# Three blocks of an MLP: the left half of the second product by seven block products in place of eight

## The chip, the core and the metric

The kernel runs on one core of one Trainium2 chip. The core has a matmul engine, TensorE (PE in the rows; its loads of stationary operands are PEld), VectorE (DVE), ScalarE (ACT), GpSimd (POOL) and SyncE (SP), whose queue issues most DMAs. Matmuls write into PSUM, which this program uses as eight banks of 128 x 512 float32; everything else lies in SBUF. Each engine takes its instructions in a fixed order and waits on semaphores for the others. The metric is the device time of one execution, in microseconds (us).

## What is computed

A two-layer encoder trunk over 256 tokens with 2048 features: in each layer attention, then a dense MLP with a squared ReLU, with 8192 hidden features.

```python
h = _rmsnorm(x) * (1.0 + sc_m) + sh_m
y = jnp.square(jax.nn.relu(h @ w_mlp_in[l])) @ w_mlp_out[l]
x = x + g_m * y
...
return _rmsnorm(x, final_norm_g)
```

The MLP of the second layer (l = 1) is the last thing before the closing norm. All values are float32.

## The kernel before

**Precision.** A float32 value is split into two float32r parts: `hi` is a rounding copy made by ACT (line 151, or 187 for activations), `lo` is the rest, which DVE makes with a subtraction (line 154, or 188). A float32 product is then three matmuls: hi x hi, hi x lo and lo x hi. Weights come from memory as float32 tiles of 128 x 2048 (`raw`, 1 MB, five buffers) and are split in two halves of 1024 columns into tiles `hi` and `lo`, which have four buffers each: a fifth half waits until the matmuls that read the first are done.

**The MLP of a layer** (end of `layer`) goes through four blocks `fb` of 2048 hidden features.

- First product: `wides` takes two tiles of 128 hidden features at a time. For each it makes 16 matmuls of 512 columns (line 217: one `hi` slice of the weights as the stationary operand, hi and lo parts of 256 tokens side by side as 512 columns), and then 16 of 256 columns (line 220: the `lo` slice on the hi parts). The two halves of the resulting bank are added by `joined` (ACT copies one, line 1201; DVE adds the other, line 1202). `relu2` applies relu and square on ACT (lines 1207 and 1208) and splits the result into `hid` (ACT line 187, DVE line 188), two tiles with hi and lo.
- Second product: `rows` computes a column of 512 output features for both halves of the tokens in two banks `pr`. It goes through four quarters `kq` of the 2048 hidden features; each is a `raw` tile and 24 matmuls of 512 columns (lines 311, 312 and 314, `hid` slices of 128 x 128 stationary, weights moving). Four columns c make a block.
- `updates` multiplies a column by the gate and adds it to x (DVE lines 1126 and 1128). In the last block of the second layer `final` does the same, sums squares on ACT (line 1142) and, after the last column, scales and stores the output.

In the second layer, block 0 has its first six hidden tiles from an earlier stage; blocks 1 to 3 are whole. All of the first product of a block comes ahead of its second product. The order of instructions on each engine is decided when the program is built, by a scheduler that starts from the order of the code; tiles take buffers from rotating pools. DMAs of weights are issued on SP's queue in the order of the code, each as soon as its buffer is free.

## Time and profile before

| | us |
|---|---|
| median of 3 runs (lowest to highest) | 2168.12 (2168.02 to 2169.72) |
| the profiled execution, its own time | 2169.38 |
| span of its trace | 2167.6 |
| first product of block 1 of the second layer | 1631.2 to 1720.1 |
| second product of that block | 1720.1 to 1807.2 |
| start of block 3 of the second layer | 1983.3 |
| last matmuls of the program | 2158 to 2159 |

A profile has one row for each group of instructions: the line of the code, the engine, the operation, the tile written <- the tiles read, shapes and count, then busy time and mean duration, then the idle time of the engine ahead of them and what ended it. A row of a timeline starts with the start in us and the length; in square brackets stands how long the engine had been idle and which instruction ended that. A row of windows gives for a stretch its length and then the busy us (and instructions) of PE, PEld, DVE, ACT and POOL, the granted clock of TensorE as a share of the full one, the busy share of the DMA engines and GB/s. Matmul durations include their latency, so successive ones overlap: their pace is read from starts.

### The profile page before, as it was taken

To read this page: it belongs to the slowest core of one execution; us is meant where nothing else is said; L and a number is where in the kernel's file an instruction comes from. 1 tells how busy PE (TensorE), PEld (TensorE's weight loads), DVE (VectorE), ACT (ScalarE), POOL (GpSimd) and SP (SyncE) were. 2 spreads that over 40 slices of the span, in tenths; PEclk is the share of its full clock that TensorE was granted. 3 is DMA by queue.
4 is the path that set the end of the run, shared out by engine and by line. 5 is a ranking of instruction groups with operands and counts; after the bars stand their busy time and mean duration, and the time that the engine had idled before them with its cause. 6 is when DMAs were issued, how large, how long until landed. Compare 5 with 4: busy or idle time off the path is not lost.

```text
span 2167.6 us, 29372 instructions
## 1 busy us (share of the span) xinstructions
PE 2140.6 (99%) x11498; PEld 1861.7 (86%) x11498; DVE 1593.9 (74%) x2122; ACT 1148.1 (53%) x1738; POOL 6.3 (0%) x18
## 2 busy tenths in 40 slices
PE   7999999999999999999999999999999999999998
PEld 6899888898888888888889998888888888888886
DVE  7888889888688888888877886778555555555555
ACT  6555663565455355445454576557535534644643
POOL 0000000000000000000000000000000000000000
PEclk9999999999999999999999999999999999999999
DMA  9998889799888988888967776767655555565552
GB/s 387 418 345 330 313 331 358 288 339 339 322 319 325 343 325 324 325 327 320 343 221 270 263 257 231 274 221 273 226 207 181 194 192 179 190 212 176 194 196 96
DMA packets 87244, 594.76 MB, mean 274 GB/s; under 512 B 9856, under 2 KB 10304, under 8 KB 20288
## 3 DMA queue, kind: packets, MB, share of 16 engines
q1 hardware_dynamic: 85968, 587.08, 73.7%
q0 software_dynamic: 848, 5.28, 0.6%
q8 instruction: 90, 1.47, 0.3%
q10 hardware_dynamic: 288, 0.52, 0.1%
q14 instruction: 50, 0.41, 0.1%
HBM read 589.66 MB, written 3.18 MB: 274 GB/s over the span
## 4 chain that ended last, share of the span: by engine, by line
PE 96%; DVE 2%; DMA 1%; ACT 1%; SPq 0%; issue 0%; ACTq 0%
PE ps L217 19%; PE pr L311 13%; PE pr L312 13%; PE pr L314 13%; PE ps L220 10%; PE pk L260 3%; PE pk L284 2%; PE pk L194 2%; PE pk L198 2%; PE pk L197 2%; PE pv L296 2%; PE pv L298 2%; PE pv L297 2%; PE psm L1372 1%; PE pk L281 1%; PE ps L197 1%
## 5 line engine op out<-in xcount | busy, mean ns | idle before, releaser
L154 DVE TENSOR_TENSOR lo<-raw,hi 128x1024 fp32r<-128x1024 f32 (+1 forms) x714 | 835.9, 1194 | 436.0 <-issue 225.2
L151 ACT ACTIVATE hi<-raw 128x1024 fp32r<-128x1024 f32 (+1 forms) x714 | 732.6, 1036 | 690.2 <-PE pr L312 365.3
L380 DVE SCALAR_TENSOR_TENSOR ada<-ada,cond 128x2048 f32<-128x2048 f32 x192 | 438.0, 2285 | 11.8 <-DMA ada<-in_w_ada 11.1
L217 PE MATMUL ps<-h,hi 128*128 128x512 f32 x1856 | 431.5, 390 | 0.0
L217 PEld LDWEIGHTS ps<-h,hi 128*128 128x128 f32 x1856 | 345.2, 188 | 69.4
L311 PE MATMUL pr<-hi,hid 128*128 128x512 f32 x1024 | 398.6, 389 | 0.0
L312 PE MATMUL pr<-hi,hid 128*128 128x512 f32 x1024 | 398.5, 389 | 0.0
L314 PE MATMUL pr<-lo,hid 128*128 128x512 f32 x1024 | 253.5, 389 | 0.0
L220 PEld LDWEIGHTS ps<-h,lo 128*128 128x128 f32 x1856 | 230.3, 192 | 4.5
L220 PE MATMUL ps<-h,lo 128*128 128x256 f32 x1856 | 231.7, 283 | 0.0
L314 PEld LDWEIGHTS pr<-lo,hid 128*128 128x128 f32 x1024 | 192.2, 188 | 39.9
L312 PEld LDWEIGHTS pr<-hi,hid 128*128 128x128 f32 x1024 | 192.2, 188 | 39.7
L311 PEld LDWEIGHTS pr<-hi,hid 128*128 128x128 f32 x1024 | 192.2, 188 | 39.7
L1201 ACT ACTIVATE sum<-ps 128x256 f32<-128x256 f32 x110 | 42.1, 383 | 114.8 <-PE ps L220 114.4
L194 PE MATMUL pk<-h,hi 128*128 128x256 f32 x320 | 90.4, 285 | 0.2 <-ACT h L705 0.2
L197 PE MATMUL pk<-h,hi 128*128 128x256 f32 x320 | 90.5, 283 | 0.0
L198 PE MATMUL pk<-h,lo 128*128 128x256 f32 x320 | 90.5, 283 | 0.0
L188 DVE TENSOR_TENSOR hid<-relu,hid 128x256 fp32r<-128x256 f32 x128 | 48.3, 421 | 49.5 <-ACT hid L187 49.5
L260 PE MATMUL pk<-hf,w 128*128 128x256 f32 x384 | 83.9, 379 | 0.0
L260 PEld LDWEIGHTS pk<-hf,w 128*128 128x128 f32 x384 | 72.8, 190 | 9.9
L194 PEld LDWEIGHTS pk<-h,hi 128*128 128x128 f32 x320 | 61.2, 192 | 0.6 <-ACT h L705 0.5
L198 PEld LDWEIGHTS pk<-h,lo 128*128 128x128 f32 x320 | 61.4, 192 | 0.2 <-DVE lo L154 0.2
(250 smaller groups left out, 2459.3 us busy)
## 6 DMA issues: line engine op xcount, KB each, us to landing
raw<-in_w_m SPq DMA_DIRECT2D x238, 1024.0 KB, 5.3
ada<-in_w_ada SPq DMA_DIRECT2D x192, 1024.0 KB, 6.4
raw<-in_w_o SPq DMA_DIRECT2D x32, 1024.0 KB, 5.5
raw<-in_w_m SPq DMA_DIRECT2D x24, 768.0 KB, 5.4
raw<-in_w_dv SPq DMA_DIRECT2D x16, 1024.0 KB, 5.5
raw<-in_w_t SPq DMA_DIRECT2D x12, 1024.0 KB, 5.8
w<-in_w_a SPq DMA_DIRECT2D x24, 384.0 KB, 13.5
raw<-in_w_a SPq DMA_DIRECT2D x12, 768.0 KB, 4.6
```

Of the source, the lines that this page charges most:

```text
L151: ins = self.nc.scalar.activation(hi, v, AF.Copy)
L154: ins = self.nc.vector.tensor_tensor(lo, v, hi.bitcast(F32), ALU.subtract)
L194: ins = mm(ps, hi, x[0], start=first, stop=False, skip_group_check=shared)
L197: mm(ps, hi, x[1], start=False, stop=False, skip_group_check=shared)
L198: self.last_mac = mm(ps, lo, x[0], start=False, stop=last, skip_group_check=shared)
L217: mm(ps.rearrange("p a b -> p (a b)"), part(w, k, 0), x[2], start=k == 0, stop=False)
L220: mm(ps[:, 0], part(w, k, 1), x[0], start=False, stop=k == nk - 1)
L260: self.nc.tensor.matmul(ps, v, whole[k], start=first, stop=last, skip_group_check=True)
L311: mm(ps, xh[:, c], part(i, 0), start=kq == 0 and i == 0, stop=False)
L312: mm(ps, xl[:, c], part(i, 0), start=False, stop=False)
L314: self.last_mm = mm(ps, xh[:, c], part(i, 1), start=False, stop=kq == 3 and i == 3)
L380: ins = nc.vector.scalar_tensor_tensor(w, w, 1.0, self.cond, ALU.mult, ALU.mult, accum_out=acc[:, i : i + 1])
```

## The change

Blocks 1 to 3 of the second layer's MLP run through a new function, `block_by_seven`. The right half of the second product (c = 2 and 3) stays as it was. The left half (c = 0 and 1), a product of tokens x hidden by hidden x 1024, is taken in blocks: two halves of the tokens, two tiles of 128 hidden features, two halves of 512 output features. A 2 x 2 by 2 x 2 block product takes eight block products as written; here it takes seven, of sums and differences of the blocks, summed over all hidden tiles in seven PSUM banks (`sums`, tiles `pp`), and `four` puts the four results together at the end of the block.

```diff
         for fb in range(NFB):
+            if l and fb:
+                self.block_by_seven(fb, h)
+                continue
...
+    def block_by_seven(self, fb, h):
+        io = self.io
+        hid, steps, sums = [], [], []
+        for m in range(0, NK, 2):
+            both = self.t("sum")
+            for j in range(2):
+                ps = self.wides([io["w_m11"][NK * fb + m + j - 6]], h)[0]
+                self.join(ps, both[:, j])
+                if steps:
+                    steps.pop(0)()
+            r = self.relu(both)
+            parts = self.split(r, "hid", True)
+            hid += parts
+            steps = self.seven(io["w_ms"][fb - 1, m // 2], parts, r, sums, m == 0, m == NK - 2)
+        for f in steps:
+            f()
+        end = fb == NFB - 1
+        for c, pss in enumerate(self.four(sums)):
+            (self.final if end else self.updates)(pss, c)
+        for c in range(2, 4):
+            pss = self.rows(io["w_m2"][1, fb], hid, c, end and c == 3)
+            (self.final if end else self.updates)(pss, c)
+
+    def seven(self, src, parts, r, sums, first, last):
...
+        s = flat(self.t("comb"))
+        (a11, a12), (a21, a22) = [[r[:, k, P * t : P * t + P] for k in range(2)] for t in range(2)]
+        q = [s[:, P * i : P * i + P] for i in range(4)]
+        add(q[2], a11, a21, ALU.subtract)
+        add(q[0], a21, a22, ALU.add)
+        add(q[1], q[0], a11, ALU.subtract)
+        add(q[3], a12, q[1], ALU.subtract)
+        hi, lo = flat(self.u("sh", F32R)), flat(self.u("sl", F32R))
+        nc.scalar.activation(hi, s, AF.Copy)
+        add(lo, s, hi.bitcast(F32), ALU.subtract)
...
+        def product(x, w, i, p):
+            ps = flat(sums[p - 1])
+            wh, wl = (v[:, 512 * i : 512 * i + 512] for v in w)
+            nc.tensor.matmul(ps, x[0], wh, start=first, stop=False)
+            nc.tensor.matmul(ps, x[0], wl, start=False, stop=False)
+            nc.tensor.matmul(ps, x[1], wh, start=False, stop=last)
+
+        def five():
+            if first:
+                sums.extend(self.bank("pp") for _ in range(7))
+            raw = self.raw(src, 2048)
+            comb = self.wp.tile([P, 2048], F32, tag="raw", name=self.name("comb"), bufs=5)
+            add(comb[:, :1024], raw[:, 512:1536], raw[:, :1024], ALU.subtract)
+            add(comb[:, 1024:1536], raw[:, 1024:1536], comb[:, :512], ALU.subtract)
+            add(comb[:, 1536:], comb[:, 1024:1536], raw[:, 1536:], ALU.subtract)
+            w = self.part(raw, 0, 512)[0]
+            product(h11, w, 0, 1)
+            w = self.part(raw, 1, 1024)[0]
+            product(h12, w, 1, 2)
+            product(s4, w, 0, 3)
+            w = self.part(comb, 0, 1024)[0]
+            product(s1, w, 0, 5)
+            product(s3, w, 1, 7)
+            st["comb"] = comb
+
+        def two():
+            w = self.part(st["comb"], 1, 1024)[0]
+            product(s2, w, 0, 6)
+            product(h22, w, 1, 4)
+
+        return [five, two]
+
+    def four(self, sums):
...
+        self.nc.scalar.activation(c11, p1, AF.Copy)
+        add(c12, p6, c11, ALU.add)
+        add(c11, p2, c11, ALU.add)
+        add(c21, p7, c12, ALU.add)
+        add(c12, p5, c12, ALU.add)
+        add(c22, p5, c21, ALU.add)
+        add(c12, p3, c12, ALU.add)
+        add(c21, c21, p4, ALU.subtract)
+        return [c11, c21], [c12, c22]
```

`joined` and `relu2` are taken apart into `join`, `relu` and `split`, and the weights of the left half are stored a second time in the new order (`w_ms`). A **step** m is one pass of the loop: the first product of two tiles, one tile at a time, with the "five" of the step before after the first tile and the "two" of the step before after the second. The last step's five and two come after the loop. Per step one `raw` tile of second-product weights is loaded, a tile `comb` of combined weights is made from it in another buffer of the same five, and four combinations of the activations are made and split (`sh`, `sl`). On PE the program has 10718 rows in place of 10790.

**A step in the middle, DVE.** Before, these rows stood around the joins of one pair of tiles in block 1 (`ps` the first product's bank, `lo` a low part of weights, `sum` the joined tile):

```order
L154 TENSOR_TENSOR lo_2722_14904<-raw_2720_14901,hi_2721_14903 128x1024
L154 TENSOR_TENSOR lo_2724_14908<-raw_2720_14901,hi_2723_14907 128x1024
L1202 SCALAR_TENSOR_TENSOR sum_2715_14886<-ps_2703_14800,sum_2715_14886 128x256
L154 TENSOR_TENSOR lo_2728_14915<-raw_2726_14912,hi_2727_14914 128x1024
L1202 SCALAR_TENSOR_TENSOR sum_2715_14886<-ps_2709_14811,sum_2715_14886 128x256
L154 TENSOR_TENSOR lo_2730_14919<-raw_2726_14912,hi_2729_14918 128x1024
```

Now, from the split of a step's combined weights to the join of the next step's second tile (`comb<-raw` is the making of the combined weights, `sl` the low part of the combined activations):

```order
L154 TENSOR_TENSOR lo_2811_15294<-comb_2805_15272,hi_2810_15293 128x1024
L1099 TENSOR_TENSOR sl_2796_15221<-comb_2794_15215,sh_2795_15220 128x512
L1295 SCALAR_TENSOR_TENSOR sum_2797_15224<-ps_2798_15225,sum_2797_15224 128x256
L154 TENSOR_TENSOR lo_2815_15307<-raw_2813_15304,hi_2814_15306 128x1024
L154 TENSOR_TENSOR lo_2817_15311<-raw_2813_15304,hi_2816_15310 128x1024
L154 TENSOR_TENSOR lo_2819_15349<-comb_2805_15272,hi_2818_15348 128x1024
L154 TENSOR_TENSOR lo_2830_15381<-raw_2828_15378,hi_2829_15380 128x1024
L1116 TENSOR_TENSOR comb_2834_15424<-raw_2833_15422 128x1024
L1117 TENSOR_TENSOR comb_2834_15424<-raw_2833_15422,comb_2834_15424 128x512
L1118 TENSOR_TENSOR comb_2834_15424<-comb_2834_15424,raw_2833_15422 128x512
L154 TENSOR_TENSOR lo_2832_15385<-raw_2828_15378,hi_2831_15384 128x1024
L1295 SCALAR_TENSOR_TENSOR sum_2797_15224<-ps_2812_15303,sum_2797_15224 128x256
```

The two joins of a pair were one row apart, with at most one split between; now eight rows of other work stand between them, and a whole step has 20 rows on DVE.

**The end of a block, ACT.** Before, at the end of block 1's first product (`hi<-raw` are splits of weights for the second product):

```order
L1201 ACTIVATE sum_2779_15286<-ps_2767_15200 128x256
L1201 ACTIVATE sum_2779_15286<-ps_2773_15211 128x256
L1207 ACTIVATE relu_2780_15291<-sum_2779_15286 128x512
L151 ACTIVATE hi_2796_15372<-raw_2795_15370 128x1024
L1208 ACTIVATE relu_2780_15291<-relu_2780_15291 128x512
L187 ACTIVATE hid_2781_15294<-relu_2780_15291 128x256
L187 ACTIVATE hid_2782_15295<-relu_2780_15291 128x256
```

Now, from the join of block 1's last tile (`pp_2681` is the first of the seven sums, `y` its copy, `sh` the high part of the combined activations):

```order
L1294 ACTIVATE sum_2855_15528<-ps_2870_15607 128x256
L151 ACTIVATE hi_2892_15713<-comb_2885_15682 128x1024
L1302 ACTIVATE relu_2878_15662<-sum_2855_15528 128x512
L1303 ACTIVATE relu_2878_15662<-relu_2878_15662 128x512
L187 ACTIVATE hid_2879_15665<-relu_2878_15662 128x256
L187 ACTIVATE hid_2880_15666<-relu_2878_15662 128x256
L1141 ACTIVATE y_2894_15723<-pp_2681_14655 128x512
L1098 ACTIVATE sh_2882_15676<-comb_2881_15671 128x512
L151 ACTIVATE hi_2905_15751<-raw_2904_15749 128x1024
```

On PE the last tile was followed by the second product's matmuls on the block's oldest `hid`; now it is followed by six matmuls of the step before and then by all 21 of the last step, on `hid_2879`, `hid_2880` and `sh_2882`, ahead of any of the right half:

```order
L1109 MATMUL pp_2684_14658<-hi_2876_15652,hid_2851_15514 128x512
L1107 MATMUL pp_2681_14655<-hi_2886_15686,hid_2879_15665 128x512
L1108 MATMUL pp_2681_14655<-lo_2887_15687,hid_2879_15665 128x512
L1109 MATMUL pp_2681_14655<-hi_2886_15686,hid_2879_15665 128x512
L1107 MATMUL pp_2682_14656<-hi_2888_15693,hid_2880_15666 128x512
L1108 MATMUL pp_2682_14656<-lo_2889_15694,hid_2880_15666 128x512
L1109 MATMUL pp_2682_14656<-hi_2888_15693,hid_2880_15666 128x512
```

Three more on `hid_2880` follow, then twelve on `sh_2882` and its low part, then the right half.

**The start of a block, ACT.** Now, from the join of block 1's second tile to the first combined activations (`hi_2698` and `hi_2700` are the two halves of the fourth tile's weights):

```order
L1294 ACTIVATE sum_2655_14500<-ps_2662_14546 128x256
L1302 ACTIVATE relu_2668_14591<-sum_2655_14500 128x512
L151 ACTIVATE hi_2694_14685<-comb_2689_14664 128x1024
L1303 ACTIVATE relu_2668_14591<-relu_2668_14591 128x512
L151 ACTIVATE hi_2698_14698<-raw_2697_14696 128x1024
L187 ACTIVATE hid_2669_14594<-relu_2668_14591 128x256
L187 ACTIVATE hid_2670_14595<-relu_2668_14591 128x256
L1294 ACTIVATE sum_2674_14609<-ps_2675_14610 128x256
L151 ACTIVATE hi_2700_14702<-raw_2697_14696 128x1024
L1098 ACTIVATE sh_2672_14605<-comb_2671_14600 128x512
```

Before, at the same place, relu, square and the two `hid` rows stood together with one split between, and nothing on PE read them until the second product. Now step 0's five, after the third tile, reads `hid_2669`, `hid_2670` and `sh_2672`.

More of the change, by code (lines that the diff above doesn't have):

```diff
@@ new lines, in four @@
+    def four(self, sums):
+        add = self.nc.vector.tensor_tensor
+        p1, p2, p3, p4, p5, p6, p7 = sums
+        c11, c12, c21, c22 = [self.t("y") for _ in range(4)]
+        self.nc.scalar.activation(c11, p1, AF.Copy)
[7 more added lines that the diff above has]
+        return [c11, c21], [c12, c22]
@@ L1199, in joined, with join, relu @@
         for i in range(2):
[L1200 to L1203 removed]
+            self.join(ps[i], out[:, i], scale)
+        return out
+    def join(self, ps, t, scale=1.0):
+        self.nc.scalar.activation(t, ps[:, 0], AF.Copy, scale=scale)
+        self.nc.vector.scalar_tensor_tensor(t, ps[:, 1], scale, t, ALU.mult, ALU.add)
     def relu2(self, ps):
+        return self.split(self.relu(ps), "hid", True)
+    def relu(self, ps):
         r = self.t("relu")
```

22 lines of the change are left out of this document (13 added, 9 removed).

## The prediction

> **What bounds the kernel now.** I read the shares of busy time first, then the chain that ended last, then the two stages that the change touches, one block of the second layer's MLP: first product from 1631.2 us, second product from 1720.1 us.
>
> ```profile
> PE 2140.6 (99%) x11498; PEld 1861.7 (86%) x11498; DVE 1593.9 (74%) x2122; ACT 1148.1 (53%) x1738; POOL 6.3 (0%) x18
> PE 96%; DVE 2%; DMA 1%; ACT 1%; SPq 0%; issue 0%; ACTq 0%
> ```
>
> ```profile
> 1631.20:1720.10 88.90, 88.90 (x514) 78.72 (x513) 49.19 (x66) 51.32 (x75) 0.00 (x0) 1.00 0.52 180
> 1720.10:1807.20 87.10, 87.10 (x386) 72.14 (x386) 46.60 (x49) 36.01 (x37) 0.00 (x0) 1.00 0.59 203
> ```
>
> In both stretches TensorE (PE) is busy for the whole time at a granted clock of 1.00, while VectorE (DVE) has 46 to 49 us of work in 87 to 89 and the DMA engines are half idle. Only matmuls taken away can save time here. Their pace stands in the chain:
>
> ```profile
> 1910.80 1.81 PE pr L314 x8
> 1916.24 1.81 PE pr L314 x8
> 1994.42 7.28 PE ps L217 x32
> 2001.70 3.83 PE ps L220 x32
> ```
>
> A quarter of a column of the second product, 24 matmuls of 512 columns, repeats every 1916.24 - 1910.80 = 5.44 us: **0.227 us each**. In the first product 512 columns take 7.28/32 = 0.2275 us and 256 columns 3.83/32 = 0.12 us, so one tile (16 + 16) takes 5.56 us.
>
> **What is removed.** The left half of the second product had 4 quarters x 24 x 2 columns = 192 matmuls a block; seven block products of three matmuls in eight steps are 168. 24 fewer in three blocks are 72 x 0.227 = **16.3 us less on PE**. All else must hide behind PE, or it comes off this.
>
> **What is added, and the middle of a block.** A step (two first-product tiles, then the "five" and "two" pieces of the seven products) takes PE 2 x 5.56 + 21 x 0.227 = 15.9 us. Durations for DVE and ScalarE (ACT):
>
> ```profile
> L154 DVE TENSOR_TENSOR lo<-raw,hi 128x1024 fp32r<-128x1024 f32 x244 | 291.8, 1220 | 249.0 <-issue 155.1 <-PE ps L220 86.9 <-ACT hi L151 7.0
> L188 DVE TENSOR_TENSOR hid<-relu,hid 128x256 fp32r<-128x256 f32 x64 | 24.2, 422 | 43.5 <-ACT hid L187 43.5
> L1202 DVE SCALAR_TENSOR_TENSOR sum<-ps,sum 128x256 f32<-128x256 f32 x58 | 24.2, 418 | 0.0
> L1128 DVE TENSOR_TENSOR x<-x,yg 128x512 f32<-128x512 f32 x33 | 21.6, 684 | 0.1
> L394 DVE TENSOR_TENSOR mod<-macc,vec 128x2 f32<-128x2 f32 x2 | 0.3, 156 | 0.0
> ```
>
> ```profile
> L151 ACT ACTIVATE hi<-raw 128x1024 fp32r<-128x1024 f32 x244 | 258.2, 1058 | 232.3 <-PE pr L312 181.3 <-PE ps L217 41.9 <-issue 5.2
> L187 ACT ACTIVATE hid<-relu 128x256 fp32r<-128x256 f32 x64 | 23.1, 410 | 0.9
> L1201 ACT ACTIVATE sum<-ps 128x256 f32<-128x256 f32 x58 | 22.3, 384 | 67.0 <-PE ps L220 66.9
> L1207 ACT ACTIVATE relu<-sum 128x512 f32<-128x512 f32 x32 | 20.2, 634 | 26.7 <-DVE sum L1202 26.7
> L1208 ACT ACTIVATE relu<-relu 128x512 f32<-128x512 f32 x32 | 19.6, 616 | 0.0
> ```
>
> The new 128-wide additions lie between 0.156 us (2 columns) and 0.422 (256); the line through both gives 0.29. The new 1024- and 512-wide subtractions are taken as L154 and L1128. A step then gives DVE seven splits and one subtraction of 1024 (9.76), four operations of 512 (2.76), four of 128 (1.16), two hid splits and two joins (1.68): **15.4 us of work in 15.9**. ACT gets seven splits, two of 512, two joins, relu, square and two hid: 11.5 us, which hides. What decides is whether DVE's operations overlap a little, and the price of a handover:
>
> ```profile
> 1701.58 0.72 ACT L187 ACTIVATE hid<-relu 128x256 fp32r<-128x256 f32 x2
> 1702.03 0.76 DVE L188 TENSOR_TENSOR hid<-relu,hid 128x256 fp32r<-128x256 f32 x2 [1.49 <-ACT hid L187]
> ...
> 1708.64 0.42 DVE L1202 SCALAR_TENSOR_TENSOR sum<-ps,sum 128x256 f32<-128x256 f32 x1
> 1708.97 1.22 DVE L154 TENSOR_TENSOR lo<-raw,hi 128x1024 fp32r<-128x1024 f32 x1
> 1709.04 7.44 PE L217 MATMUL ps<-h,hi 128*128 128x512 f32 x32
> 1709.24 0.38 ACT L1201 ACTIVATE sum<-ps 128x256 f32<-128x256 f32 x1 [1.54 <-PE ps L220]
> 1710.11 0.42 DVE L1202 SCALAR_TENSOR_TENSOR sum<-ps,sum 128x256 f32<-128x256 f32 x1
> ```
>
> DVE starts 1.14 us after a 1.22 us split began and 0.33 after a 0.42 us join: 0.08 less than the duration. ACT to DVE costs 0.04 (1701.58 + 0.41 to 1702.03). ACT reads a finished tile 0.20 us after PE has gone on (1709.04 to 1709.24).
>
> The seven sums hold seven of PSUM's eight banks, so a tile can start only when the join before it has emptied the last bank. From the start of a step's first tile: split buffers rotate by four, so the split of the combined weights waits for the buffer that this tile's low parts free at 3.64 + 0.96 + 0.20 = 4.80 us. With it twelve DVE operations stand up to the join of the second tile (their rows are in the part on the change): seven of 1.22, three of 0.69, two joins, 11.45 us end to end, 10.8 with nine overlaps of 0.08 and two dependent steps of 0.04. The join ends at 15.6, PE may go on at 15.7, and at full pace it wants to at 15.9. So I cost the middle at **nothing, with 0.2 us to spare**. In the first two joins of a block a 512 split stands ahead of the join: by the same sum 0.15 + 0.1 us late, 0.7 us in three blocks. End to end it would be 16.35, so 0.48 us late in each step.
>
> [...]
>
> **The two ends of a block**, where nothing lies between a step's relu and its products.
>
> ```profile
> 1452.87 0.16 DVE L1159 RECIPROCAL rms<-rms 128x1 f32<-128x1 f32 x1 [0.51 <-ACT rms L1156]
> 1453.08 0.30 PEld L1163 LDWEIGHTS pn<-ident,rms 128*128 128x128 f32 x2 [0.18 <-DVE rms L1159]
> ...
> 2097.46 1.98 PE L314 MATMUL pr<-lo,hid 128*128 128x512 f32 x8
> 2097.72 1.06 ACT L151 ACTIVATE hi<-raw 128x1024 fp32r<-128x1024 f32 x1 [0.20 <-PE pr L312]
> ```
>
> PE starts loading 0.05 us after its releaser, and I add 0.1 for the load that is no longer hidden. ACT takes a buffer freed by a 512-column matmul 0.26 us after PE's next one began.
>
> End, from the last tile's end: the "two" of the step before runs to 1.36. ACT's order puts the split of the last combined weights ahead of relu, and its buffer is free at 1.62: split to 2.68, relu 3.23, square 3.89, hid 4.34. PE's first product starts at 4.5, **3.1 us after its last matmul's slot**. It waits again for hid's low part (DVE 4.80, PE 4.96); nine matmuls are done at 6.55. The combined activations' split stands on ACT behind the copy of the first sum, which waits for that product, and is ready at 6.59; twelve matmuls from 6.75 end at about 9.55. At full pace it is 1.36 + 21 x 0.227 = 6.13. **Loss 3.4 us.**
>
> Start, from the first tile: tiles end at 5.56, 11.12, 16.68. The second join waits behind a split whose buffer the second tile frees, and ends at 12.88; relu, a split, square, a split and hid follow on ACT to 16.4 and 16.7, the low parts on DVE at 17.71 and 18.05. Then the split for the next tile's second half, waiting for the buffer of product one (18.36 to 19.42), stands ahead of the combined activations (19.95). PE takes them at 20.1 and has nine matmuls left: 22.15, at full pace 20.08. **Loss 2.1 us.**
>
> If no operation waited for a buffer, the same chains would lose 1.7 and 1.1 us; if each of some eight links cost 0.1 more, 4.2 and 2.9. I take 3.4 and 2.1, since the order's rows and the rotation by four give them. After the end DVE has seven sums, eight updates and four splits up to the third quarter's low weights: 15 x 0.69 + 4 x 1.22 = 15.2 us end to end, 13.8 with the overlaps. The last is due after two quarters, 16 matmuls and a half low part, 10.9 + 3.6 + 0.9 = 15.4 us, so PE's column hides them and I cost them at nothing; each tenth that they grow beyond it would come off PE.
>
> **The clock.** PE never waits in these stages today, so what a 3 us wait does is read elsewhere:
>
> ```profile
> 215.05 0.39 PE L194 MATMUL pss<-lath,hi 128*128 128x256 f32 x1 [2.12 <-ACT hi L151]
> ...
> 216.31 0.58 PE L198 MATMUL pss<-lath,lo 128*128 128x256 f32 x1 [0.51 <-DVE lo L154]
> ```
>
> ```profile
> 214.00:216.00 2.00, 0.75 (x4) 0.53 (x4) 0.96 (x1) 1.95 (x3) 0.00 (x0) 1.00 0.72 295
> 216.00:218.00 2.00, 1.69 (x8) 1.69 (x9) 2.00 (x3) 0.00 (x0) 0.00 (x0) 0.57 0.07 29
> 218.00:220.00 2.00, 2.00 (x12) 2.00 (x12) 2.00 (x3) 0.00 (x0) 0.00 (x0) 0.58 0.80 217
> 220.00:222.00 2.00, 2.00 (x19) 2.00 (x19) 1.89 (x3) 0.80 (x2) 0.00 (x0) 1.00 0.99 410
> ```
>
> A wait of 2.12 us and one of 0.51 were followed by 4 us at 0.57 and 0.58: up to 4 x 0.43 = 1.7 us lost. The wait at a block's end is longer, with PE mostly bound after it. I take 1.5 us at two of the three ends, **3.0 us**; the bounds are none, and 1.7 at each of the three ends.
>
> [...]
>
> **Sum.** -16.3 + 3 x (3.4 + 2.1) + 0.7 + 3.0 = **+3.9 us**. The profiled execution took 2169.38 us (span 2167.6), 1.3 above the median of 2168.12; on its own time that is 2173.3, on the median **2172.0**.
>
> **Rivals.**
> - DVE sets the pace. If its operations run end to end, each step is 0.48 us late: 7 steps x 3 x 0.48 = 10 us more, 2182. For it: 15.4 us of work in 15.9, and a spare of 0.2. Against: the 0.08 us overlaps. It decides once the twelve operations take over 11.0 us. Chance 0.17. [...]
> - The ends cost half, and it is faster: the buffers that I read as waited for are free when ACT reaches them, so relu is not held. Then 3 x (1.7 + 1.1) = 8.4, PE's wait stays under 2 us and the clock stays up: 2168.1 - 16.3 + 8.4 = 2160.2. It decides where both ends of a block lose under (16.3 - 4.3)/3 = 4.0 us. Against: today's splits wait on PE for 181.3 us in L151's row, as the rotation has it. Chance 0.16.
> - The waits are as forecast, but the clock holds: +0.9, 2169.0. [...] Against: the 2.12 us row. Chance 0.12. [...]
>
> **How the numbers follow.** The forecast has 0.55, from 2169 to 2176. A measurement of this kernel can tell about 0.2% (4.3 us: 2163.8 and 2172.5) from no change. Of the forecast 0.32 lies within and 0.23 above; the rival on DVE is slower (0.17), the one with free buffers faster (0.13, and 0.03 within), the one on the clock within (0.11, and 0.01 above). Faster 0.13, same 0.46, slower 0.41. The range, 2163 to 2182, leaves out about half of each outer rival.
>
> **What would show it.** Right: PE idle for about 3 us before the first product of a block's last step, put down to ACT's hid, and about 2 us in pieces at step 0's products; granted clock below 1 after the former; steps of 15.9 us in between; 72 matmuls fewer. Wrong: middle tiles that wait on DVE's join in every step (steps of 16.3 us), or waits at the ends of under 1.5 us, or the backlog after a block's end making PE wait for low weights.

## The result, and the profile after

| | before | after |
|---|---|---|
| median (lowest to highest), 6 runs each | 2168.49 us (2168.02 to 2169.72) | 2176.59 us (2173.86 to 2179.35) |
| ratio, 95% interval | | 1.0034 [1.0023, 1.0044] |
| the profiled execution, and its span | 2169.38, 2167.6 | 2175.54, 2173.8 |

The changed kernel is slower by 0.34%, 7.4 us of the 2169 that a run of the kernel before takes. The forecast was 3.9 us slower, and the time lies inside its range of 2163 to 2182. The page of the changed kernel starts with the busy times:

```profile
PE 2133.1 (98%) x11426; PEld 1848.3 (85%) x11426; DVE 1744.9 (80%) x2383; ACT 1201.8 (55%) x1813; POOL 6.2 (0%) x18
```

The 72 matmuls are gone (11426 for 11498), and PE is busy for 7.5 us less than before, not 16.3: others ran longer. The share of PE falls from 99 to 98% while the span grows, so time went into waits. Where they are is seen with the block cut at the first matmul of its right half. Before, in block 1, from the first tile to the end of the left half, and the right half:

```profile
1631.28:1763.68 132.40, 132.40 (x705) 114.78 (x704) 72.02 (x89) 70.34 (x96) 0.00 (x0) 1.00 0.55 191
1763.68:1807.22 43.54, 43.54 (x193) 36.04 (x192) 23.72 (x25) 16.98 (x16) 0.00 (x0) 1.00 0.56 193
```

The same windows after, and then the stretches behind the last tile of blocks 1, 2 and 3 in which the matmuls are slow:

```profile
1629.95:1764.82 134.87, 130.50 (x681) 111.17 (x680) 112.20 (x161) 86.82 (x120) 0.00 (x0) 0.99 0.52 189
1764.82:1808.34 43.52, 43.52 (x193) 36.04 (x192) 33.88 (x40) 18.52 (x18) 0.00 (x0) 1.00 0.54 189
1758.00:1761.60 3.60, 3.28 (x8) 2.60 (x9) 2.01 (x7) 2.17 (x5) 0.00 (x0) 0.54 0.93 332
1936.00:1939.10 3.10, 2.78 (x7) 2.20 (x8) 1.56 (x6) 1.67 (x5) 0.00 (x0) 0.50 0.93 309
2113.90:2120.10 6.20, 6.09 (x14) 4.78 (x15) 3.26 (x7) 2.56 (x6) 0.00 (x0) 0.50 0.72 264
```

The right half is what it was, 43.52 us for 43.54. The left part has 24 matmuls fewer (681 for 705) and takes 134.87 us where 132.40 - 24 x 0.227 = 126.95 was to be had. So block 1 loses 7.9 us in its left part; blocks 2 and 3, whose left parts take 134.23 and 135.66, lose 7.3 and 8.7. The sum is 23.9 us, less the 16.3 saved: **7.6 us slower by the trace**, and 7.4 by the ratio.

PE's waits from 1480 us on (engine, tile, line <- who ended the wait: us in all, times, longest), and below them one row of the waits of PE's loads:

```profile
PE pp L1107 <- ACT hid L187: 8.5, 3, 2.8
PE pp L1107 <- ACT sh L1098: 4.0, 3, 1.3
PE pp L1109 <- DVE hid L188: 0.2, 1, 0.2
```

```profile
PEld ps L217 <- DVE sum L1295: 2.4, 6, 0.4
```

All four are waits that the prediction named: `hid` at the three ends, `sh` at the three starts, `hid`'s low part at one start, the join (`sum`) at two tiles a block. What releases `hid` and `sh` late is on ACT: at all three ends and all three starts a split (L151) stands ahead in ACT's queue that itself waits for PE to free a buffer. The first row is from the end of block 1, the other two from its start:

```profile
1755.58 1.06 ACT L151 ACTIVATE hi<-comb 128x1024 fp32r<-128x1024 f32 x1 [1.05 <-PE pp L1109]
...
1648.62 1.06 ACT L151 ACTIVATE hi<-raw 128x1024 fp32r<-128x1024 f32 x1 [1.42 <-PE pp L1109]
1649.58 0.61 ACT L1098 ACTIVATE sh<-comb 128x512 fp32r<-128x512 f32 x1
```

The end of block 1 on PE, from its last matmul on work of the step before to the first of the right half:

```profile
1755.11 0.39 PE L1109 MATMUL pp<-hi,hid 128*128 128x512 f32 x1
1758.32 0.79 PE L1107 MATMUL pp<-hi,hid 128*128 128x512 f32 x1 [2.83 <-ACT hid L187]
1758.91 0.63 PE L1108 MATMUL pp<-lo,hid 128*128 128x512 f32 x1
...
1761.05 0.63 PE L1107 MATMUL pp<-hi,hid 128*128 128x512 f32 x1
...
1761.83 0.40 PE L1109 MATMUL pp<-hi,hid 128*128 128x512 f32 x1
...
1764.82 0.39 PE L311 MATMUL pr<-hi,hid 128*128 128x512 f32 x1
```

Seven matmuls behind the wait start 0.43 us apart in place of 0.23: the granted clock is 0.50 for 3.41 us (1758.30 to 1761.71). In these rows there is no wait for the combined activations: `sh` is ready at 1761.12 us on ACT, and the slow matmuls keep PE from them until 1762.06. At the third end 14 matmuls are slow.

A step in the middle on DVE, the start and the end of its chain of twelve operations:

```profile
1696.61 1.23 DVE L154 TENSOR_TENSOR lo<-comb,hi 128x1024 fp32r<-128x1024 f32 x1 [0.54 <-PE ps L220]
1697.75 0.69 DVE L1099 TENSOR_TENSOR sl<-comb,sh 128x512 fp32r<-128x512 f32 x1
...
1706.95 0.42 DVE L1295 SCALAR_TENSOR_TENSOR sum<-ps,sum 128x256 f32<-128x256 f32 x1
```

The step's first tile started at 1691.76. The split starts 4.85 us later, released by PE's low slice (`ps` L220), and the second join ends at 1707.37, 15.61 us after the tile; the forecast had 4.80 and 15.6. PE's next step starts at 1707.65, after 15.89 us.

### The profile page after: what moved, and what is told of

Its sections match the earlier page's. It is cut to its first block, busy times and chain, and to the rows that moved or that the text cites. A ratio compares the mean times of both kernels' runs of the same rounds, so it can differ in the third digit from the quotient of the medians.

```text
span 2173.8 us, 29544 instructions
## 1 busy us (share of the span) xinstructions
PE 2133.1 (98%) x11426; PEld 1848.3 (85%) x11426; DVE 1744.9 (80%) x2383; ACT 1201.8 (55%) x1813; POOL 6.2 (0%) x18
## 4 chain that ended last, share of the span: by engine, by line
PE 95%; DVE 2%; ACT 2%; DMA 1%; issue 0%; SPq 0%; ACTq 0%
PE ps L217 19%; PE pr L311 11%; PE pr L312 11%; PE pr L314 11%; PE ps L220 10%; PE pk L260 3%; PE pk L284 2%; PE pp L1107 2%; PE pp L1108 2%; PE pp L1109 2%; PE pk L194 2%; PE pk L198 2%; PE pk L197 2%; PE pv L296 2%; PE pv L298 2%; PE pv L297 2%
## 5 line engine op out<-in xcount | busy, mean ns | idle before, releaser
L151 ACT ACTIVATE hi<-raw 128x1024 fp32r<-128x1024 f32 (+2 forms) x714 | 722.6, 1022 | 640.5 <-PE pr L312 283.3
L154 DVE TENSOR_TENSOR lo<-raw,hi 128x1024 fp32r<-128x1024 f32 (+2 forms) x714 | 823.8, 1176 | 302.6 <-issue 121.8
L217 PE MATMUL ps<-h,hi 128*128 128x512 f32 x1856 | 435.9, 390 | 0.0
L311 PE MATMUL pr<-hi,hid 128*128 128x512 f32 x832 | 323.9, 389 | 0.0
L312 PE MATMUL pr<-hi,hid 128*128 128x512 f32 x832 | 323.7, 389 | 0.0
L220 PEld LDWEIGHTS ps<-h,lo 128*128 128x128 f32 x1856 | 233.5, 191 | 6.4
L220 PE MATMUL ps<-h,lo 128*128 128x256 f32 x1856 | 235.5, 283 | 0.0
L314 PE MATMUL pr<-lo,hid 128*128 128x512 f32 x832 | 206.1, 389 | 0.0
L314 PEld LDWEIGHTS pr<-lo,hid 128*128 128x128 f32 x832 | 156.2, 188 | 32.4
L312 PEld LDWEIGHTS pr<-hi,hid 128*128 128x128 f32 x832 | 156.2, 188 | 32.3
L311 PEld LDWEIGHTS pr<-hi,hid 128*128 128x128 f32 x832 | 156.1, 188 | 32.3
L154 DVE TENSOR_TENSOR lo<-comb,hi 128x1024 fp32r<-128x1024 f32 x48 | 58.6, 1221 | 10.5 <-PE ps L220 6.1
```

The lines of the kernel that those rows point to most:

```text
L151: ins = self.nc.scalar.activation(hi, v, AF.Copy)
L154: ins = self.nc.vector.tensor_tensor(lo, v, hi.bitcast(F32), ALU.subtract)
L217: mm(ps.rearrange("p a b -> p (a b)"), part(w, k, 0), x[2], start=k == 0, stop=False)
L220: mm(ps[:, 0], part(w, k, 1), x[0], start=False, stop=k == nk - 1)
L311: mm(ps, xh[:, c], part(i, 0), start=kq == 0 and i == 0, stop=False)
L312: mm(ps, xl[:, c], part(i, 0), start=False, stop=False)
```

## The experiments

All times are medians, and each ratio is to runs of the kernel before on the same chip (its medians there were 2169.73, 2169.57 and 2169.22). The fourth column is the loss of the left parts of the three blocks in the profiled execution, as worked out above (sum of the times from a block's first tile to its right half, less 3 x 126.95). The fifth adds what the right halves take over those of the changed kernel and takes off 16.3: what the trace makes of the kernel against before. The last is the ratio's answer, in us of 2169.

| kernel | median (lowest to highest, runs) | ratio, 95% interval | loss, left | net by trace | net by ratio |
|---|---|---|---|---|---|
| changed | 2176.59 (2173.86 to 2179.35, 6) | 1.0034 [1.0023, 1.0044] | 23.9 | +7.6 | +7.4 |
| e_warm | 2172.18 (2171.12 to 2174.5, 11) | 1.0013 [1.0004, 1.0022] | 18.8 | +2.5 | +2.8 |
| e_warm4 | 2176.32 (2171.26 to 2178.71, 8) | 1.0027 [1.0017, 1.0037] | 20.2 | +3.9 | +5.9 |
| e_start | 2168.80 (2165.63 to 2171.5, 11) | 0.9996 [0.9987, 1.0005] | 16.2 | -0.1 | -0.9 |
| e_start_warm | 2165.16 (2163.26 to 2167.75, 11) | 0.9979 [0.997, 0.9987] | 12.5 | -3.8 | -4.6 |
| e_swap | 2174.17 (2173.27 to 2178.28, 7) | 1.0029 [1.0018, 1.004] | 23.6 | +7.3 | +6.3 |
| e_all | 2172.87 (2170.8 to 2178.2, 11) | 1.0018 [1.0009, 1.0027] | 13.9 | +2.8 | +3.9 |
| e_act_end | 2179.07 (2177.99 to 2182.27, 5) | 1.0044 [1.003, 1.0058] | 20.5 | +8.7 | +9.5 |
| e_start_end | 2172.41 (2170.4 to 2175.08, 11) | 1.0014 [1.0006, 1.0023] | 14.3 | +4.5 | +3.0 |
| e_dve | 2176.64 (2174.16 to 2178.88, 7) | 1.0031 [1.002, 1.0041] | 21.3 | +5.0 | +6.7 |
| e_one | 2171.28 (2167.53 to 2173.85, 11) | 1.0003 [0.9994, 1.0012] | | | +0.7 |
| e_eight | 2172.97 (2169.21 to 2173.7, 11) | 1.0012 [1.0003, 1.0021] | | | +2.6 |

The last two columns, one worked out from a single profiled execution and one from all runs, stay within 2 us of each other: what a kernel gains or loses here is in these stretches. A line number of an experiment can be some more than in the changed kernel, since its edit moves the code below it.

### The clock: e_warm

```diff
+        for _ in range(12):
+            self.last_warm = self.nc.tensor.matmul(flat, self.zero, h[0][2], start=False, stop=False)
+            self.behind(self.last_warm, self.last_pp)
         for f in steps:
             f()
```

Ahead of the last step's products, twelve matmuls with a stationary operand of zeros add nothing to the sixth sum while PE would wait.

> Twelve matmuls of 512 columns with a stationary operand of zeros are added into one of the seven sums at each block's end, between the two pieces, where PE had waited 2.8 us for hid. If the half clock after that wait costs what the trace of the change shows (nine matmuls at 0.43 us in place of 0.23, so that 21 take from 4.37 to 10.87 us after the last tile, where the walk at full clock gave 9.55), the clock stays at 1 and each end gets 1.3 us shorter: 4.0 us less than the change, about 2172.5 beside 2176.6, and less spread between runs. If the low clock costs nothing, because the products would have waited for the combined activations anyway, the time stays at that of the change.

The end of block 1 on PE, and the clock of the first and the third end in windows of 21 us (the second has 1.00 too):

```profile
1756.88 2.88 PE L1081 MATMUL pp<-h,zero 128*128 128x512 f32 x12
1759.87 0.50 PE L1114 MATMUL pp<-hi,hid 128*128 128x512 f32 x1
1760.21 0.40 PE L1117 MATMUL pp<-lo,hid 128*128 128x512 f32 x1
```

```profile
1752.00:1773.00 21.00, 20.89 (x99) 16.91 (x98) 17.70 (x27) 13.28 (x17) 0.00 (x0) 1.00 0.78 281
...
2107.00:2128.00 21.00, 20.89 (x99) 16.89 (x98) 17.79 (x26) 13.18 (x17) 0.00 (x0) 1.00 0.76 273
```

The products start no earlier, but the second starts 0.34 us after the first and the others follow 0.23 us apart, at a clock of 1.00, and the kernel is 1.0034 - 1.0013 = 0.0021, 4.6 us, faster than the changed one (the two intervals leave some 3 us either way). That is the price of the clock, apart from the wait itself. With the clock held, each end takes 9.47 us from the last tile to the right half in place of 10.87, 10.62 and 12.12: the profiled execution of the changed kernel paid 1.4 + 1.15 + 2.65 = 5.2 us.

### The start: e_start, and both: e_start_warm

```diff
+                order = (self.last_sh, None) if (m, j) == (2, 1) else None
...
+        last_q = add(q[3], a12, q[1], ALU.subtract)
+        self.last_sh = nc.scalar.activation(hi, s, AF.Copy)
...
+            w = self.part(comb, 0, 1024, last_q if first else None)[0]
```

On ACT the splits of the fourth tile's weights stand behind the split of the first combined activations (`sh`); on DVE the low part of the first combined weights stands behind the combinations of the activations.

> Only the order on two engines changes, at the start of each block: ACT splits the fourth tile's weights behind the combined activations of step 0, and DVE makes the low part of the combined weights behind those sums. If the 1.34 us wait at the start is due to the split that stands ahead (it waits for the buffer of product one), the wait falls to under 0.3 us and the start loses about 0.8 us where it lost 2.4: 3 x 1.6 = 4.8 us less than the change, about 2172. If the wait was due to DVE's total work instead, it only moves to the next tile or to the next step, and the time stays.

The waits of PE from 1480 us on are down to one row, and the products on `sh` follow those on `hid` after 0.48 us:

```profile
PE pp L1108 <- ACT hid L187: 8.5, 3, 2.8
```

```profile
1650.87 0.39 PE L1110 MATMUL pp<-hi,hid 128*128 128x512 f32 x1
1651.35 0.50 PE L1108 MATMUL pp<-hi,sh 128*128 128x512 f32 x1
```

The order of ACT and DVE was the whole of that wait; which of the two matters more the run doesn't tell, since it changes both. The gain, 0.0038 or 8.2 us (some 3 us either way), is larger than the 4.8 that were expected. By the trace, which makes it 7.7, the five of step 0 take 3.99, 3.62 and 3.64 us in place of 5.77, 5.45 and 5.43, which is 5.4 us in three blocks; of the two steps behind it the second takes 15.9 in place of 16.2, 0.9 us more; and the rest is the clock, which happened to slow 20 matmuls of this execution and 27 of the changed kernel's.

> Both parts together: the order of ACT and DVE at a block's start as in e_start, and twelve zero matmuls into the sixth sum in PE's wait at a block's end as in e_warm. Theory: the losses are independent, the reorder takes the start's wait away and the zero matmuls keep the clock. e_start's profile still had three slow stretches after the ends, of 7, 7 and 6 matmuls at 0.43 us apart in place of 0.23, about 4.0 us in all; without them 2165 on the scale of e_start's 2168.8, ratio to the kernel before 0.998, and no wait of PE in its rows from 1620 us on. Rival: the timed executions of e_start were slowed less than its profiled one (its 11 runs reach from 2165.6 to 2171.5); then the gain is 1 to 2 us, 2167 to 2168, ratio 0.9990 to 0.9996.

Both edits together, and no row of PE's waits is left after 1620 us. The gains add up: 1.0034 - 0.0021 - 0.0038 = 0.9975, measured 0.9979. This version is **faster than both kernels**, by 0.21% [0.13, 0.30] against before. So the seven products do pay here, but only with both of their edges mended; the 12.5 us that its left parts still lose are three ends of 3.3 us, 1.0 us at the starts, and late joins.

### The end: e_swap, e_act_end, e_start_end, e_all

Four attempts to make the wait at the ends shorter, not only harmless. In e_swap the pieces of the last step but one are cut the other way: six matmuls after the first tile of the last step, fifteen after its second.

```diff
-        return [five, two]
+        return [six, fifteen] if swap else [five, two]
```

> In the last pass of a block the six matmuls stand after the first tile and the fifteen after the second, so that 3.4 us of work in place of 1.36 lie between the last tile and the last step's products. If the loss at the end is the chain join, relu, square, hid and not something in the products, PE's wait falls from 2.8 us to about 1, the clock stays at 1, and each end gets 2.0 + 1.3 = 3.3 us shorter: 10 us less than the change, about 2166.5, 2 us under the kernel before. If the two weights buffers that are now held longer delay DVE as much as PE gains, the time stays within 2 us of the change.

```profile
PE pp L1107 <- ACT sh L1098: 6.0, 6, 1.3
PE pp L1107 <- ACT hid L187: 5.1, 3, 1.7
PE ps L217 <- DVE sum L1317: 2.7, 3, 0.9
```

The wait for `hid` fell only from 2.8 to 1.7 us, with 9 more matmuls, 2.0 us, behind the last tile. On ACT three splits (at block 1's end they start at 1758.73, 1760.21 and 1761.68) now stand between the join's copy and `hid`, where the changed kernel has one, and `hid` starts 4.62 us after the last tile in place of 3.90. `sh`, which the slow clock had hidden, is now waited for at the ends (six times for three), and DVE, which has to make all of the combined weights ahead of the six, ends a tile's join 0.9 us late. By the ratio 1.1 us came of it, less than the two intervals can tell, where 10 were expected.

In e_act_end, ACT's order at a block's end is changed: behind `sh` stand the split of the last combined weights, the copy of the first sum, and the right half's first split.

```diff
+            w = self.part(st["comb"], 1, 1024, None, self.last_sh if last else None)[0]
...
+        self.behind(self.nc.scalar.activation(c11, p1, AF.Copy), self.last_sh)
...
+            order = (self.last_sh, None) if c == 2 else None
+            pss = self.rows(io["w_m2"][1, fb], hid, c, end and c == 3, order)
```

> Only the order on ACT at a block's end: relu, square and hid, then the combined activations, and behind them the split of the last combined weights, the copy of the first sum and the right half's first split. relu then starts at 2.0 us after the last tile in place of 2.6: the wait for hid falls from 2.8 to about 2.2 us, too little to keep the clock up (a wait of 2.12 us was followed by 0.57 in the kernel before). 0.6 to 1.0 us less at each end, 2 to 3 us less than the change, about 2174. If the clock does stay up, 6 to 7 us less.

```profile
PE pp L1108 <- ACT hid L187: 6.8, 3, 2.3
PE pp L1108 <- ACT sh L1099: 4.3, 4, 1.3
PE pr L314 <- DVE lo L154: 3.9, 2, 1.9
```

The wait for `hid` is 0.55 us shorter, three times. More did not come of it because relu, no longer behind the split, now waits for DVE's join, which ends at 1757.30 behind a split of DVE's own. And behind two of the ends a new wait of 1.9 us stands in the right half: the kernel is no faster than the changed one (1.0044 for 1.0034), where 2 to 3 us less were expected. I first put that down to the held split of the right half. e_start_end leaves it out and takes the start's order along:

> e_start, and at a block's end the split of the last combined weights and the copy of the first sum behind the split of the combined activations on ACT; the splits for the right half stay where the order had them (in e_act_end one of them was held back too, and the right half's low weights came late). Theory: hid is ready about 0.5 us earlier (2.28 us of wait in place of 2.83, as in e_act_end), the combined activations wait for nothing, and the split that is put off is due only after fifteen matmuls: 1.5 us off in three ends, and somewhat more where the shorter wait keeps the clock: 2165.5 to 2167.5 beside e_start's 2168.8. Rival: what is put off on ACT comes late elsewhere, as the right half's low weights did in e_act_end (3.9 us over two blocks): then 2169 to 2172, with a wait at the right half's products in the rows.

```profile
PE pp L1108 <- ACT hid L187: 6.8, 3, 2.3
PE pr L314 <- DVE lo L154: 4.3, 2, 2.3
PE pp L1108 <- ACT sh L1099: 0.3, 1, 0.3
```

The rival of the expectation came: a wait in the right half, and 2172.4 us. Since the wait is there all the same, the held split was not its cause. DVE's rows behind the second end show what is (a row of x2 is two operations), with PE's row below:

```profile
1949.63 1.29 DVE L1217 TENSOR_TENSOR yg<-y,bias 128x512 f32<-128x512 f32 x2
...
1953.25 1.28 DVE L1219 TENSOR_TENSOR x<-x,yg 128x512 f32<-128x512 f32 x2
1954.45 2.35 DVE L154 TENSOR_TENSOR lo<-raw,hi 128x1024 fp32r<-128x1024 f32 x2
```

```profile
1955.72 1.20 PE L314 MATMUL pr<-lo,hid 128*128 128x512 f32 x4 [1.94 <-DVE lo L154]
```

The split at 1954.45 is the right half's fourth, the low part of the second half of its second quarter. In the order of the changed kernel four of the right half's splits stand ahead of the eight updates (here 1949.63 to 1954.45), and PE has no wait there. Here the split of the last combined weights has moved down behind `sl`, on DVE as on ACT, and the scheduler let only three more in ahead of the updates. So the fourth came 4.8 us of updates late, and PE waited 1.9 us for it. The third block mixes updates and splits, and has no such wait. e_all, which joins the start's order, the swap and e_act_end's order, has the same three splits and met the same wait.

> The new order at the start, the six and fifteen in the last pass, and at the end on ACT the split of the last combined weights, the copy of the first sum and the right half's first split behind the combined activations. The start would lose 0.8, the middle 0.7 as in the trace of the change, the end about 1.3 (0.6 until hid, 0.6 until the combined activations): 3 x 2.8 = 8.4 against 16.3 us of matmuls saved, so about 2160.5, 8 us under the kernel before. If there is a loss that the three places don't hold, the time stays above 2165.

```profile
PE pr L314 <- DVE lo L154: 4.6, 2, 2.3
PE pp L1109 <- ACT sh L1100: 3.1, 3, 1.0
PE ps L217 <- DVE sum L1319: 2.7, 3, 0.9
PE pp L1109 <- ACT hid L187: 2.7, 3, 0.9
```

Its left parts lose only 13.9 us, 2.3 us less than e_start's, and the right halves give 5.2 back, 4.6 of it these waits: 2172.9 us where 2160.5 were expected. An end that is shorter and has the fourth split in its place was not tried.

### DVE's spare: e_dve

The low part `sl` is made twice in every step.

> Every step makes the low part of the combined activations twice, one more DVE operation of 0.69 us (0.61 with the overlap) in the chain to the second join. If DVE's chain ends 0.1 to 0.2 us before PE wants the bank, as forecast, each step gets about 0.5 us longer: steps of 16.4 us, 6 to 7 of them in three blocks, 9 to 11 us more than the change, about 2187. If DVE had more to spare (over 0.6 us a step), the middle stays at 15.9 to 16.1 and the time rises by under 2 us, at the ends.

The time did not move, so the expectation failed. The trace shows why. In every second step the scheduler put the first of the two `sl` ahead of the chain, where DVE has idle time, so that the chain still has twelve operations; there the time from one second join to the next is 15.8 us. In the other steps it has thirteen. There the split starts and the join ends the chain so:

```profile
1714.47 1.23 DVE L154 TENSOR_TENSOR lo<-comb,hi 128x1024 fp32r<-128x1024 f32 x1 [0.41 <-PE ps L220]
...
1725.37 0.41 DVE L1296 SCALAR_TENSOR_TENSOR sum<-ps,sum 128x256 f32<-128x256 f32 x1
```

That is 11.31 us for thirteen, where the changed kernel took 10.76 for twelve. Those joins come after 16.39 to 16.54 us in place of 15.83 to 15.9, which is 0.5 us late: one operation of 0.69 us uses up the spare. From the second join of a block to its last this makes 113.5 us for the 112.7 of the changed kernel, 2.5 us in three blocks. In the table 21.3 us of loss stand against e_warm's 18.8, the same 2.5, both at full clock; the medians can't show so little. That the execution profiled was at full clock is the other finding of this run, below.

### One block, and eight products

e_one has only the last block changed, `if l and fb == 3`.

> Only block 3 of the second layer goes by seven, blocks 1 and 2 as before. If each block carries the same loss (start 2.4, middle 0.7, end 4.7, less 5.4 us of matmuls), the time is a third of the change's excess: +2.4 to +2.7 us, about 2171. If the excess came from the change from one block to the next, or from the code that grew, it is near 0 or near the whole.

A third of 0.0034 is 0.0011, and the interval of 0.9994 to 1.0012 takes it in, as it does no change: the medians don't tell. The trace does: it has one wait of 2.82 us for `hid` and one of 1.3 for `sh`, and the block's left part takes 134.47 us, a loss of 7.5 beside the 7.3 to 8.7 of the changed kernel's blocks. So each block carries its own loss.

e_eight keeps the interleaving but makes all eight block products, in four sums, without any combinations:

```diff
-                sums.extend(self.bank("pp") for _ in range(7))
+                sums.extend(self.bank("pp") for _ in range(4))
...
+            w = self.part(raw, 0, 1024)[0]
+            product(h11, w, 0, 0, True, False)
+            product(h11, w, 1, 1, True, False)
+            product(h21, w, 0, 2, True, False)
+            product(h21, w, 1, 3, True, False)
```

> The same interleaving with all eight block products: 24 matmuls a step on four sums, no combined weights or activations, so DVE has 5 us less a step and PE 0.68 us more. It tells the price of the interleaving from that of the seven. If the loss is the chain from the last tile to hid and the clock after it, the end still loses about 3 + 1.3 us and the start about 0.5 (hid alone): about 3 x 4.8 = 14 us over the kernel before, 2183. If the loss comes from the sums and differences that the seven need, the time is near that of the kernel before, 2168 to 2171.

I had the ends and starts cost as much here as with seven; they cost almost nothing. PE's only wait from 1620 us on is 0.2 us. With four sums three more banks are free, and the scheduler lets PE start the right half where it would wait:

```profile
1758.80 0.39 PE L1097 MATMUL pp<-hi,hid 128*128 128x512 f32 x1
1759.03 0.39 PE L311 MATMUL pr<-hi,hid 128*128 128x512 f32 x1
...
1762.78 0.51 PE L1095 MATMUL pp<-hi,hid 128*128 128x512 f32 x1
```

Between the step before and the last step's products stand 16 matmuls of the right half, which fill 3.75 us. So the interleaving of the two products by itself costs 2.6 us by the ratio, and 2.0 by the trace (its three blocks take 530.0 us for 528.0 before). The waits come with the three more sums and the combinations, and this run takes both away at once. That it is the banks, seven of eight taken, which leave PE nothing else to run meanwhile is an argument from the code; no run tried them alone.

### How short a wait is short enough: e_warm4

e_warm with `range(4)`: a third of the filling.

> The changed kernel with four zero matmuls, not twelve, in PE's wait at a block's end: about 1.0 us of the 2.83 is filled, so that PE idles 1.9 us in one piece. Theory, from when the slow stretches begin and end in the runs so far: the clock is judged by stretches of about 3.4 us that lie on a grid of their own, and the next stretch is slowed when the one before has some 2.0 us or more of idle time (2.83 us that the grid cut so that one stretch held at most 1.9 were followed by none in e_dve; 2.28 us were followed by a slow stretch at two of three ends in e_act_end). Then 1.9 us can slow nothing wherever the grid lies: granted clock 1.00 after all three ends, and the time of e_warm, about 2172 or 4 us below the changed kernel. Rival: any wait over about 1.7 us can be followed by a slow stretch (e_swap's 1.71 were not); then at least one of three ends is slow and the time lies between, about 2174.

The expectation failed. The waits are 1.92 us, the clock is 1.00 behind the first two ends (the first is shown), and behind the third it is not:

```profile
1758.00:1764.00 6.00, 5.93 (x25) 4.56 (x26) 4.62 (x9) 4.79 (x8) 0.00 (x0) 1.00 0.57 202
...
2111.90:2115.20 3.30, 3.30 (x9) 2.58 (x9) 1.97 (x5) 2.06 (x3) 0.00 (x0) 0.51 0.95 320
```

The profiled execution, 2171.63 us, is also one of the fastest of the eight, which reach from 2171.3 to 2173.5 (three) and from 2176.1 to 2178.7 (five), where the eleven of e_warm lie from 2171.1 to 2174.5. Filling a third of the wait is not a safe third of the gain.

## Why the prediction came out as it did

The forecast gave 0.55 to times from 2169 to 2176. From the 2168.1 that it started from, the ratio makes 2175.5, at the upper edge, and the median itself, 2176.6, lies just above. Of its three outcomes, slower had 0.41 and no change 0.46. Step by step, in the profiled execution of the changed kernel:

| term | forecast, us | measured, us |
|---|---|---|
| 72 matmuls fewer | -16.3 | -16.3 |
| three starts | 3 x 2.1 = 6.3 | 2.4 + 2.0 + 2.0 = 6.5 |
| middle | 0.7 | 0.7 + 0.7 + 0.6 = 2.0 |
| three ends at full clock | 3 x 3.4 = 10.2 | 3 x 3.34 = 10.0 (e_warm: 9.47 less 6.13) |
| the clock | 3.0 | 5.2 (4.6 by the medians of e_warm) |
| sum | +3.9 | +7.4 |

A start is measured from a block's first tile to its fourth (22.50, 22.12 and 22.10 us against the 20.08 at full pace), an end from its last tile to the right half, and the middle is what lies between (101.5 us for 5.56 + 6 x 15.87 = 100.8).

- **What bounds the kernel** held: where nothing stops PE it keeps the pace of before (steps of 15.89 us), so that the matmuls taken away count with their full 0.227 us each, and everything lost is time in which PE waits or is slowed.
- **The ends and starts** were right in cause and place, and as sums in size. The walk along the queues had the last products start 4.5 us after the last tile, and 2.1 us lost at the start in pieces; the trace has 4.37 us, and 0.2 + 1.3 + 0.6 (the last in PE's loads). The rival "the ends cost half" is refuted by its own sign: both ends of a block together lose 5.4 to 5.8 us at full clock, not under 4.0. The choice on which it hung fell as forecast, since ACT's rows show the splits waiting for their buffers. But what moving those splits away is worth was put wrong. The walk had 1.1 us for a start without them and 1.7 for an end; e_start, which moves the waiting splits away, gains 1.8 us a start and not 1.0, while e_act_end gains 0.55 us of the wait for `hid` at an end and not 1.7, since another wait stands behind.
- **The middle** was right in mechanism: twelve operations, join at 15.6, steps of 15.89. The rival "DVE sets the pace" is refuted by those steps, and e_dve's thirteen operations show how near it was. The changed kernel's twelve don't run end to end: they take 10.76 us (1696.61 to 1707.37) where the walk had 11.45 for that, and the splits at 1700.96 and 1702.10 us start 1.14 us apart and last 1.22. The two joins behind a 512 split came 0.31 and 0.34 us late, where I had 0.15 and 0.1: the term of 0.7 us was mis-sized by 1.3.
- **The clock** was the term that was mis-sized most. "I take 1.5 us at two of the three ends" should have been three ends, one of them for two stretches in a row: 5.2 us against 3.0, past the bound of 5.1. How much of it an execution pays is in part luck: the rival "the clock holds" is refuted for this execution, but in that of e_dve, with the same waits, it is what happened, since each wait fell across two stretches with at most 1.95 us of idle time in one (below).
- **The backlog behind an end**, costed at nothing with four splits counted in it, did hide in the changed kernel. e_act_end and e_start_end show the price when one of those splits falls behind the updates: waits of 3.9 and 4.3 us, and right halves that are 4.5 and 6.5 us longer.

The two mis-sized terms make 2.2 + 1.3 = 3.5 us, which is the whole difference between the two sums; the starts' 0.2 too little and the ends' 0.2 too much cancel.

## What to carry to other kernels

Fewer matmuls only pay by what their edges leave: where a new product depends on the last result of another stage, walk every queue from that result to the matmul, and count how many PSUM banks are left for something else to run meanwhile. Waits on PE that left 2.05 us or more of idle time in one stretch of 3.41 us had to be priced twice here, once for themselves and once for the clock, and the second price changed from one profiled execution to another (5.2 us in the changed kernel's, none in e_dve's with the same waits); either fill them entirely, as the twelve matmuls on zeros did for 4.6 us, or don't have them. And a piece of the chain that is made faster moves the wait to the next piece without a reserve, here DVE's join and its backlog of sums, which the list of waits doesn't show before.

## What the runs showed of the clock

That the same wait does not always slow PE was not expected. Of the waits of 2.83 us, all three of the changed kernel, all three of e_start and the one of e_one were followed by a slow stretch; none of the three of e_dve was, in rows that look the same up to the wait:

```profile
1760.96 0.50 PE L1108 MATMUL pp<-hi,hid 128*128 128x512 f32 x1 [2.83 <-ACT hid L187]
1761.29 0.40 PE L1109 MATMUL pp<-lo,hid 128*128 128x512 f32 x1
```

Of the waits of 2.28 us (e_act_end, e_start_end) four of six were, of those of 1.92 us (e_warm4) one of three, of those of 1.71 us (e_swap) none of three. The slow stretch of block 1 in the changed kernel begins at 1758.30 us, as its wait ends (1758.32); the one behind a wait of 2.31 us in e_start_end begins about 1.3 us after it. The three of the changed kernel last 3.41, 3.41 and 6.83 us, and its first matmuls at full pace start at 1761.83, 1939.36 and 2120.14 us, that is 177.5 and 180.8 us apart: 52.0 and 53.0 times 3.41. So the slow stretches of this trace lie on a grid of 3.41 us, and the grid's place decides how much of a wait falls into one of its stretches.

The granted clock bears that out: it is 0.50 from 1758.30, 1935.79 and 2113.29 us on, 52.0 times 3.413 us apart. Two neighbouring stretches of the grid in the changed kernel, the one with the wait at the end of block 1 and the one behind it:

```profile
1754.89:1758.30 3.41, 0.61 (x3) 0.18 (x1) 2.69 (x5) 2.65 (x5) 0.00 (x0) 1.00 0.98 375
1758.30:1761.71 3.41, 3.39 (x8) 2.71 (x9) 1.82 (x6) 1.98 (x4) 0.00 (x0) 0.50 0.93 332
```

In all thirteen traces, from 1620 to 2150 us, wherever the clock is 0.50 it is so for one such stretch of 3.413 us or for two. Count each matmul of 512 columns as 0.227 us of work from its start, one of 256 as half of that, and the rest of a stretch as idle. Then each of the 15 stretches with 2.05 us or more of idle time was followed by one at half clock, and none of the others was, of which the idlest has 2.01. So the line lies near 2.0 us of 3.41 in these traces. Idle time counted so is longer than a wait in the profile, which counts from the reported end of the last matmul, 0.39 us after its start. e_dve's three waits were each cut in two by the grid, with at most 1.95 us in one stretch. The one of e_warm4 that was followed by half clock lay whole in a stretch with 2.20 us of idle time, and that is why its expectation failed. Other waits fit too: one of 2.31 us in the right half of block 1 in e_start_end, and two of 0.21 and 1.32 us at the start of block 1 in e_swap, in one stretch with 2.19 us of idle time, were followed by half clock. No run set the grid, so the line is read from where it happened to lie.
